# Grouping two pairs of row tiles in a one-core fused QKV projection: bf16 products together, float32r products together

## The chip, the cores and the metric

The kernel runs on one core of one Trainium2 chip. The metric is device time in microseconds (us) of one execution; the kernel before takes 360.74 us (median of 3 runs, 360.47 to 361.23). TensorE multiplies, VectorE, ScalarE and GpSimd (DVE, ACT and POOL in the profile) prepare operands and move results, and SyncE (SP) only issues DMAs.

## The reference

```python
batch, seq, hidden = 16, 512, 768          # x: 16 x 512 x 768, w_qkv: 768 x 2304, float32
qkv = np.matmul(x, w_qkv)
q, k, v = qkv[..., :768], qkv[..., 768:1536], qkv[..., 1536:]
return np.stack([q, k, v], axis=0)
```

So it is one matrix product of 8192 x 768 by 768 x 2304, whose columns go to three outputs.

## The kernel before, in words

**Tiling.** The 8192 rows of x are 64 row tiles of 128 rows. Two neighbouring row tiles form a pair (`p`, 0 to 31). The 2304 columns are two blocks of 1024 columns and, between them, a remainder of 256 columns (`REM`). A `Quad` is one pair times one of the two 1024-column blocks (`q` = 0 or 1): a 2 x 2 arrangement of 128 x 512 output tiles c11, c12, c21, c22, kept in one SBUF tile `o`.

**Seven products instead of eight.** Each quad is computed by one level of Strassen's scheme in Winograd's form: the inner size 768 is cut into two halves of 384, and seven half-size products are made, each of three matmuls (384 = 3 x 128) with 512 columns. Products 1 and 2 use x and w themselves, rounded to bf16 (`xb`, `b1`). Products 3 to 7 use sums and differences, in float32r (`sr` for x, `t1` to `t4` and `b22` for w). The remainder is done directly, in bf16, with twelve matmuls of 256 columns per pair (`rem`, L304; `rem_row`, L297). So a pair has twelve bf16 matmuls of 512 columns, twelve of 256, and thirty float32r matmuls of 512.

**One product and what follows it (`do`, L255).** Product 1 starts PSUM bank `u.x`, and ACT copies it out (`evacuate`, L253) while the bank stays in use; product 2 goes to bank `u.z`, which DVE adds to c11 (L266); product 6 accumulates into `u.x`, and ACT copies c12 (L269); product 5 starts bank `u.y`; product 7 accumulates into `u.x`, ACT copies c22 (L275) and DVE adds `u.y` (L276); product 4 accumulates into `u.x`, ACT copies c21 (L279); product 3 accumulates into `u.y`, which DVE adds to c12 (L282). There are 8 PSUM banks.

**Order of the work.** The schedule is written by hand: every engine runs its instructions in the order in which the program names them. After a start-up part (pairs 0 to 2 and the preparation of w), the loop at L602 takes pairs 3 to 31 one by one. For each pair `two` (L318) makes, for its quads a and b, in this order: a1, b1, `early()`, the remainder, a2, b2, a6, b6, a5, a7, b5, b7, a4, a3, store of a, b4, b3, store of b. `early` prepares the next pair (`ahead`, L486): `transpose` on DVE (L148, instruction at L154), `round_x` on POOL (L189, L191: the bf16 copy), `sums_x` on POOL (L204: five operations); then it issues the x load of the pair after that (`load_x`, L142): four DMAs, two on SP's queue and, from pair 5 on, two on ACT's queue (L129). Pair 31 goes through `last` (L360), whose products and stores are interleaved and which stores each quad in pieces (`store_cols`, L347) as they become ready, most on SP's queue and some on ACT's.

**Buffers that matter.** `o` tiles: 5; x as loaded (`xin`): 3; x transposed (`xf`): 2; bf16 x (`xb`): 4; sums of x (`s`): 2. One more quad-sized tile, `both`, holds w data at the start and later quad u2 (pair 2, second block, L598). Stores of a quad (`store_quad`, L287) are two DMAs on SP's queue (L289 and L290, or L293 and L294); the remainder's store is one (L314). In the built program every DMA issued from SP or ACT carries one of eight semaphores in turn, and waits until the DMA eight places earlier has landed.

Of the kernel before, what the change touches and what calls it, by code (L numbers as in the profile page):

```python
# [10 lines left out]
def kernel(  # L11
# [20 lines left out]
    nc = tc.nc  # L32
    P = 128
    G = 32
# [7 lines left out]
    NP = M // (2 * P)  # L42
# [18 lines left out]
    bt_pool = ctx.enter_context(tc.tile_pool(name="bt", bufs=1))  # L61
# [22 lines left out]
    both = bt_pool.tile([P, 2, KH * CB], fp32, name="both", tag="both")  # L84
# [41 lines left out]
    def load_x_half(p, h, eng):  # L126
        rows = x_flat[p * 2 * P:(p + 1) * 2 * P, :].rearrange("(g b) k -> b g k", b=G)
        for i in (2 * h, 2 * h + 1):
            eng.dma_start(xin[p][i * G:(i + 1) * G], rows[:, :, i * KC:(i + 1) * KC])  # L129
# [12 lines left out]
    def load_x(p, other):  # L142
        xin[p] = xin_pool.tile([P, 2 * P // G, KC], fp32, name="xin")
        load_x_half(p, 0, nc.sync)
        if other is not None:
            load_x_half(p, 1, other)

    def transpose(p, parts=1):  # L148
        t = xf_pool.tile([P, KT, 2 * P], fp32, name="xf")
        turned = t[:].rearrange("p j (g b) -> p g j b", b=G)  # L150
        rows = xin.pop(p)[:].rearrange("p g (a j) -> p g j a", a=G)
        n = 2 * P // G // parts
        for g in range(0, 2 * P // G, n):
            nc.vector.transpose(turned[:, g:g + n], rows[:, g:g + n])  # L154
        xf[p] = t

# [32 lines left out]
    def round_x(p):  # L189
        xb[p] = xb_pool.tile([P, KT, 2 * P], bf16, name="xb", tag="xb")  # L190
        nc.gpsimd.tensor_copy(out=xb[p][:], in_=xf[p][:])  # L191
# [12 lines left out]
    def sums_x(p, eng=None):  # L204
        t = xf.pop(p)
        a11, a12 = t[:, :KH, :P], t[:, KH:, :P]
        a21, a22 = t[:, :KH, P:], t[:, KH:, P:]
        s = s_pool.tile([P, 5, KH, P], f32r, name="s")
        sr[p] = s
        sums = {  # L210
            1: lambda g: g.tensor_tensor(s[:, 1], a21, a22, op=add),  # L211
            2: lambda g: g.tensor_tensor(s[:, 2], s[:, 1], a11, op=sub),  # L212
            3: lambda g: g.tensor_tensor(s[:, 3], a11, a21, op=sub),  # L213
            0: lambda g: g.tensor_copy(out=s[:, 0], in_=a22),
            4: lambda g: g.tensor_tensor(s[:, 4], a12, s[:, 2], op=sub),  # L215
        }
# [32 lines left out]
    def bank():  # L249
        return ps_pool.tile([P, CB], fp32, name="ps")  # L250

    def evacuate(u):
        nc.scalar.activation(u.o[:, 0, :CB], u.x[:], ident)  # L253

    def do(u, n, out=True):  # L255
        c11, c12 = u.o[:, 0, :CB], u.o[:, 0, CB:]
        c21, c22 = u.o[:, 1, :CB], u.o[:, 1, CB:]
        if n == 1:
            u.x = bank()
            product(u, 1, u.x, True)  # L260
            if out:
                evacuate(u)
        elif n == 2:
            u.z = bank()
            product(u, 2, u.z, True)
            nc.vector.tensor_tensor(c11, c11, u.z[:], op=add)  # L266
        elif n == 6:
            product(u, 6, u.x, False)
            nc.scalar.activation(c12, u.x[:], ident)  # L269
        elif n == 5:  # L270
            u.y = bank()
            product(u, 5, u.y, True)
        elif n == 7:
            product(u, 7, u.x, False)
            nc.scalar.activation(c22, u.x[:], ident)  # L275
            nc.vector.tensor_tensor(c22, c22, u.y[:], op=add)  # L276
        elif n == 4:
            product(u, 4, u.x, False)
            nc.scalar.activation(c21, u.x[:], ident)  # L279
        elif n == 3:  # L280
            product(u, 3, u.y, False)
            nc.vector.tensor_tensor(c12, c12, u.y[:], op=add)  # L282

    def rows_of(s, p, lo, hi):
        return out_flat[s, p * 2 * P:(p + 1) * 2 * P, lo:hi].rearrange("(r m) n -> m r n", m=P)

    def store_quad(u):  # L287
        if u.q == 0:
# [15 lines left out]
    def rem(p, eng=nc.sync, between=None):  # L304
        ps = ps_pool.tile([P, 2, REM], fp32, name="ps")
        rem_row(p, 0, ps[:, 0, :])
        if between is not None:
            between()
        rem_row(p, 1, ps[:, 1, :])

        def copied():
            o = or_pool.tile([P, 2, REM], fp32, name="orem")
            act.activation(o[:], ps[:], ident)  # L313
            return lambda: eng.dma_start(rows_of(1, p, R_OFF - H, R_OFF - H + REM), o[:])  # L314

        return copied

    def two(a, b, early, u=None):  # L318

        do(a, 1)  # L320
        do(b, 1, u is None)
        if u is None:
            early()
            rem(a.p)()()
        else:
            middle(u)
            copied = rem(a.p, between=lambda: third(u))
            evacuate(b)
            early()
            copied()()  # L330
            fourth(u)
        do(a, 2)
        do(b, 2)
        do(a, 6)
        do(b, 6)
        do(a, 5)
        do(a, 7)
        do(b, 5)
        do(b, 7)
        do(a, 4)  # L340
        do(a, 3)
        store_quad(a)
        do(b, 4)
        do(b, 3)
        store_quad(b)

    def store_cols(u, r, lo, hi, eng):  # L347

        c = Q_OFF[u.q] + lo
        end = Q_OFF[u.q] + hi  # L350
        while c < end:
            n = min(end, (c // H + 1) * H)
            row = (2 * u.p + r) * P
            eng.dma_start(  # L354
                out_flat[c // H, row:row + P, c % H:c % H + n - c],
                u.o[:, r, c - Q_OFF[u.q]:n - Q_OFF[u.q]],
            )
            c = n

    def last(a, b):  # L360

        p = a.p

        def rem_stored(r):
            ps = bank()
            rem_row(p, r, ps[:, :REM])
            o = or_pool.tile([P, 2, REM], fp32, name="orem")
            nc.scalar.activation(o[:, 0, :], ps[:, :REM], ident)  # L368
            row = (2 * p + r) * P
            nc.scalar.dma_start(out_flat[1, row:row + P, R_OFF - H:R_OFF - H + REM], o[:, 0, :])  # L370

        do(a, 1)
        do(b, 1)
        do(a, 2)
        do(a, 6)
        do(b, 2)
        do(b, 6)
        for u in (a, b):
            store_cols(u, 0, 0, CB, nc.sync)
        for u in (a, b):  # L380
            do(u, 5)
            do(u, 7)
            store_cols(u, 1, CB, 2 * CB, nc.sync)
        do(a, 4)
        store_cols(a, 1, 0, CB, nc.scalar)
        rem_stored(0)
        do(b, 4)
        store_cols(b, 1, 0, CB, nc.scalar)
        for u in (a, b):
            do(u, 3)  # L390
            store_cols(u, 0, CB, 2 * CB, nc.sync)
        rem_stored(1)


    ND = 2
# [21 lines left out]
    for h in range(2):  # L417
        rows = w_qkv.rearrange("(p j) n -> p j n", j=KT)[:, h * KH:(h + 1) * KH]
# [17 lines left out]
    quads = {}  # L436
# [34 lines left out]
    def middle(u):  # L471
        do(u, 6)
        do(u, 5)
        act.activation(u.o[:, 1, CB:], u.y[:], ident)
# [7 lines left out]
    def fourth(u):  # L482
        do(u, 4)
        store_quad(u)

    def ahead(p):  # L486
        transpose(p)
        round_x(p)
        sums_x(p)
# [7 lines left out]
    turned = [turn_row(0, 0)]  # L497
# [57 lines left out]
    u = quad(2, 0)  # L555
# [42 lines left out]
    u2 = quad(2, 1, bt_pool, "both")  # L598
    do(u2, 1)
    do(u2, 2)  # L600

    for p in range(ND + 1, NP):  # L602
        def early():
            if p + 1 < NP:
                ahead(p + 1)
            if p + 2 < NP:
                load_x(p + 2, nc.sync if p <= ND + 2 else nc.scalar)

        a, b = quad(p, 0), quad(p, 1)
        if p == ND + 1:  # L610
            two(a, b, early, u2)
        elif p < NP - 1:
            two(a, b, early)
        else:
            last(a, b)


# [28 lines left out]
```

## Time and profile before

| What | Value |
|---|---|
| median of 3 runs | 360.74 us (360.47 to 361.23) |
| the profiled execution's own time | 361.78 us |
| its span (first to last instruction) | 360.0 us |
| granted TensorE clock | 1.00 throughout |
| PE busy | 351.5 us (98%) |
| DVE, ACT, POOL busy | 227.8, 185.9, 178.8 us |
| HBM read, written | 32.28 MB, 75.50 MB |
| share of the 16 DMA engines' time: SP's queue, ACT's queue | 82.5%, 8.9% |

Busy shares are averages over the span. A matmul's end in the trace is modelled, and matmuls overlap: the distance from the start of one matmul to the start of the next is what it costs, not its duration (a 128x512 matmul lasts 379 to 399 ns in the groups, and another starts some 0.22 us later). A few matmul records are missing from the trace. "PEld" is TensorE's weight load, which runs beside the matmul before it. In a timeline, neighbouring equal instructions are merged into one row: its start, its length, and how many they are.

### The profile page before, as it was taken

Reading aid. Unit: us, or ns where it says so; the run is one execution under the profiler, and the core shown is the slowest. Engines: PE = TensorE matmul, PEld = TensorE weight load, DVE = VectorE, ACT = ScalarE, POOL = GpSimd, SP = SyncE. Lnnn points to the kernel's source line nnn. Section 1 sums busy time; section 2 is a strip of 40 time slices with the busy share of each in tenths; the row PEclk is TensorE's granted clock in tenths of the full one; section 3 lists DMA queues with packets and bytes.
Section 4 is the critical chain, followed back from the end, with each engine's and each line's share of the span. In section 5 each row is a group of like instructions: output and inputs, shape, how many; then the busy total and the mean of one; then the engine's idle time right before and its main releaser. Section 6 shows DMA issues by size and latency. Waiting matters only on the chain.

```text
span 360.0 us, 5248 instructions
## 1 busy us (share of the span) xinstructions
PE 351.5 (98%) x1749; PEld 251.4 (70%) x1780; DVE 227.8 (63%) x244; ACT 185.9 (52%) x316; POOL 178.8 (50%) x187
## 2 busy tenths in 40 slices
PE   7999999999999999999999999999999999999995
PEld 3465577777777777777777777777777777777764
DVE  2789676766566675566675566675556676556643
ACT  5469744545454545454545444455444445545443
POOL 0221856446664445665445665444665444665420
PEclk9999999999999999999999999999999999999999
DMA  7999999799998999899999899998999999989767
GB/s 265 340 367 345 325 357 371 236 333 298 275 325 301 295 276 290 282 319 301 292 285 284 284 309 309 292 285 282 290 295 315 293 295 272 297 283 322 291 238 257
DMA packets 82106, 107.73 MB, mean 299 GB/s; under 512 B 5408, under 2 KB 62240, under 8 KB 82080
## 3 DMA queue, kind: packets, MB, share of 16 engines
q1 hardware_dynamic: 66672, 96.35, 82.5%
q10 hardware_dynamic: 14608, 10.65, 8.9%
q0 software_dynamic: 800, 0.39, 0.8%
q8 instruction: 14, 0.23, 0.3%
q14 instruction: 12, 0.10, 0.1%
HBM read 32.28 MB, written 75.50 MB: 299 GB/s over the span
## 4 chain that ended last, share of the span: by engine, by line
PE 92%; DMA 5%; issue 1%; ACT 1%; ACTq 0%; POOL 0%; SPq 0%
PE ps L244 78%; PE ps L299 11%; PE ps L456 3%; DMA w_rem<-in_w_qkv_dram 2%; DMA xin<-in_x_dram 2%; DMA st<-in_w_qkv_dram 1%; ACT o L279 0%; ACTq L354 0%; POOL w_rem L419 0%; SPq L163 0%; ACT orem L368 0%; POOL mark L414 0%; ACTq L370 0%; ACTq L368 0%
## 5 line engine op out<-in xcount | busy, mean ns | idle before, releaser
L244 PE MATMUL ps<-t,s 128*128 128x512 f32 x720 | 181.2, 399 | 0.0
L244 PEld LDWEIGHTS ps<-t,s 128*128 128x128 f32 x720 | 135.0, 188 | 30.7
L191 POOL CAST xb<-xf 128x1536 bf16<-128x1536 f32 x28 | 41.0, 1464 | 132.2 <-DVE xf L154 132.2
L276 DVE TENSOR_TENSOR o<-o,ps 128x512 f32<-128x512 f32 x58 | 39.9, 688 | 91.5 <-ACT o L275 91.5
L154 DVE STREAM_TRANSPOSE xf<-xin 128x1536 f32<-128x1536 f32 (+1 forms) x32 | 88.7, 2775 | 1.7 <-DMA xin<-in_x_dram 1.7
L244 PE MATMUL ps<-b,xb 128*128 128x512 bf16 x331 | 85.3, 380 | 1.5
L244 PEld LDWEIGHTS <-xb 128*128 128x128 bf16 x360 | 32.8, 98 | 37.3 <-issue 7.6
L269 ACT ACTIVATE o<-ps 128x512 f32<-128x512 f32 x60 | 36.0, 600 | 43.6 <-PE ps L244 40.9
L275 ACT ACTIVATE o<-ps 128x512 f32<-128x512 f32 x58 | 34.7, 599 | 44.2 <-PE ps L244 44.2
L282 DVE TENSOR_TENSOR o<-o,ps 128x512 f32<-128x512 f32 x60 | 41.3, 688 | 21.4 <-PE ps L244 20.2
L244 PE MATMUL ps<-b,s 128*128 128x512 f32 x180 | 50.4, 389 | 0.0
L279 ACT ACTIVATE o<-ps 128x512 f32<-128x512 f32 x60 | 35.9, 598 | 24.6 <-PE ps L244 21.7
L253 ACT ACTIVATE o<-ps 128x512 f32<-128x512 f32 x60 | 35.8, 597 | 24.4 <-DVE o L282 20.7
L299 PE MATMUL ps<-w_rem,xb 128*128 128x256 bf16 x384 | 47.5, 273 | 0.6 <-DMA w_rem<-in_w_qkv_dram 0.6
L299 PEld LDWEIGHTS <-xb 128*128 128x128 bf16 x384 | 37.2, 98 | 12.3 <-issue 1.8
L266 DVE TENSOR_TENSOR o<-o,ps 128x512 f32<-128x512 f32 x60 | 37.8, 672 | 2.0 <-ACT o L253 1.3
L244 PEld LDWEIGHTS ps<-b,s 128*128 128x128 f32 x180 | 33.8, 188 | 7.1
L211 POOL TENSOR_TENSOR s<-xf 128x384 fp32r<-128x384 f32 x29 | 30.9, 1065 | 0.0
L212 POOL TENSOR_TENSOR s<-s,xf 128x384 fp32r<-128x384 f32 x29 | 29.4, 1015 | 2.3
L213 POOL TENSOR_TENSOR s<-xf 128x384 fp32r<-128x384 f32 x29 | 29.5, 1017 | 0.0
L215 POOL TENSOR_TENSOR s<-xf,s 128x384 fp32r<-128x384 f32 x29 | 29.5, 1017 | 0.0
L313 ACT ACTIVATE orem<-ps 128x512 f32<-128x512 f32 x31 | 18.5, 598 | 21.0 <-PE ps L299 21.0
(45 smaller groups left out, 119.3 us busy)
## 6 DMA issues: line engine op xcount, KB each, us to landing
out_dram<-o SPq DMA_DIRECT2D x62, 768.0 KB, 4.6
out_dram<-o SPq DMA_DIRECT2D x65, 256.0 KB, 4.0
xin<-in_x_dram SPq DMA_DIRECT2D x62, 192.0 KB, 6.9
xin<-in_x_dram ACTq DMA_DIRECT2D x50, 192.0 KB, 4.3
out_dram<-orem SPq DMA_DIRECT2D x31, 256.0 KB, 5.8
st<-in_w_qkv_dram SPq DMA_DIRECT2D x11, 256.0 KB, 5.6
st<-in_w_qkv_dram SPq DMA_DIRECT2D x3, 768.0 KB, 9.2
xin<-in_x_dram SPq DMA_DIRECT2D x4, 384.0 KB, 4.7
```

The source lines that it names most:

```text
L154: nc.vector.transpose(turned[:, g:g + n], rows[:, g:g + n])
L191: nc.gpsimd.tensor_copy(out=xb[p][:], in_=xf[p][:])
L211: 1: lambda g: g.tensor_tensor(s[:, 1], a21, a22, op=add),
L244: nc.tensor.matmul(ps[:], lhs[j], rhs[j], start=(start and j == 0), stop=(j == KH - 1), skip_group_check=True,)
L253: nc.scalar.activation(u.o[:, 0, :CB], u.x[:], ident)
L266: nc.vector.tensor_tensor(c11, c11, u.z[:], op=add)
L269: nc.scalar.activation(c12, u.x[:], ident)
L275: nc.scalar.activation(c22, u.x[:], ident)
L276: nc.vector.tensor_tensor(c22, c22, u.y[:], op=add)
L279: nc.scalar.activation(c21, u.x[:], ident)
L282: nc.vector.tensor_tensor(c12, c12, u.y[:], op=add)
L299: nc.tensor.matmul(ps, xb[p][:, j, r * P:(r + 1) * P], w_rem[j // KH][:, j % KH, :], start=(j == 0), stop=(j == KT - 1), skip_group_check= ...
```

## The change

From pair 6 on, two pairs form a group (13 groups: pairs 6 and 7, up to 30 and 31). A group makes all bf16 work of both pairs first (products 1 and 2 and the remainders), then the float32r products of the first pair's quads, then those of the second pair's. The group's first quad takes the tile `both`, the other three take `o` tiles. The order of the float32r products inside a pair stays as it was (`rounded`, the second half of the former `two`).

x is loaded four and five pairs ahead in a group (two pairs ahead before), always with all four DMAs on SP's queue. So that the first group finds its data, pair 3 loads two pairs' x (5 and 6), pair 4 loads x of pair 7, pair 5 loads x of 8 and 9, and pair 5 also does the transpose of pair 7, in two halves put between the stores and additions of its float32r products, and its rounding. Inside a group the transposes and roundings of the next two pairs stand in the bf16 part, and `sums_x` runs for the group's second pair at the group's start and for the next group's first pair in the middle.

In the last group the remainder of pair 31 stays at the end, in `last`; products 1 and 2 leave `last`, and so do the places of products 6: they now stand one after the other. The first store pieces of pair 31 come before them in the program.

The core of the diff:

```diff
-    def two(a, b, early, u=None):
+    def two(a, b, early, u=None, turns=()):
...
         do(a, 2)
         do(b, 2)
+        rounded(a, b, turns)
+
+    def rounded(a, b, turns=()):
         do(a, 6)
         do(b, 6)
         do(a, 5)
         do(a, 7)
         do(b, 5)
         do(b, 7)
+        for t in turns[:1]:
+            t()
         do(a, 4)
         do(a, 3)
         store_quad(a)
+        for t in turns[1:]:
+            t()
         do(b, 4)
         do(b, 3)
         store_quad(b)
...
-        do(a, 1)
-        do(b, 1)
-        do(a, 2)
-        do(a, 6)
-        do(b, 2)
-        do(b, 6)
         for u in (a, b):
             store_cols(u, 0, 0, CB, nc.sync)
+            do(u, 6)
...
+    def group(p):
+        quads = [quad(p, 0, bt_pool, "both"), quad(p, 1)]
+        do(quads[0], 1)
+        do(quads[1], 1)
+        sums_x(p + 1)
+        if p + 2 < NP:
+            transpose(p + 2)
+            round_x(p + 2)
+        if p + 4 < NP:
+            load_x(p + 4, nc.sync)
+        rem(p)()()
+        do(quads[0], 2)
+        do(quads[1], 2)
+        quads += [quad(p + 1, q) for q in range(2)]
+        do(quads[2], 1)
+        do(quads[3], 1)
+        if p + 5 < NP:
+            load_x(p + 5, nc.sync)
+        if p + 2 < NP:
+            rem(p + 1)()()
+        do(quads[2], 2)
+        do(quads[3], 2)
+        if p + 3 < NP:
+            transpose(p + 3)
+            round_x(p + 3)
+        rounded(*quads[:2])
+        if p + 2 < NP:
+            sums_x(p + 2)
+            rounded(*quads[2:])
+        else:
+            last(*quads[2:])
...
-        if p == ND + 1:
-            two(a, b, early, u2)
-        elif p < NP - 1:
-            two(a, b, early)
-        else:
-            last(a, b)
+    NG = ND + 4
+    extra = {NG - 3: (NG, ), NG - 1: (NG + 3, )}
+    for p in range(ND + 1, NG):
+        late_turns = []
+        def early():
+            ahead(p + 1)
+            for n in (p + 2 + (p > NG - 3), ) + extra.get(p, ()):
+                load_x(n, nc.sync)
+            if p == NG - 1:
+                late_turns.extend(transpose(NG + 1, 2, True))
+        two(quad(p, 0), quad(p, 1), early, u2 if p == ND + 1 else None, late_turns)
+        if p == NG - 1:
+            round_x(NG + 1)
+    for p in range(NG, NP, 2):
+        group(p)
```

`transpose(p, 2, True)` returns the two half transposes as functions, to be called later.

More of the change, by code (lines that the diff above doesn't have):

```diff
@@ L146, in load_x, with transpose @@
             load_x_half(p, 1, other)
-    def transpose(p, parts=1):
+    def transpose(p, parts=1, split=False):
         t = xf_pool.tile([P, KT, 2 * P], fp32, name="xf")
@@ L152, in transpose @@
         n = 2 * P // G // parts
-        for g in range(0, 2 * P // G, n):
-            nc.vector.transpose(turned[:, g:g + n], rows[:, g:g + n])
+        turns = [
+            lambda g=g: nc.vector.transpose(turned[:, g:g + n], rows[:, g:g + n])
+            for g in range(0, 2 * P // G, n)
+        ]
         xf[p] = t
+        if split:
+            return turns
+        for turn in turns:
+            turn()
     def load_row(p, r):
@@ L600 @@
     do(u2, 2)
-    for p in range(ND + 1, NP):
-        def early():
[L604 to L609, printed above, removed]
-        if p == ND + 1:
-            two(a, b, early, u2)
-        elif p < NP - 1:
-            two(a, b, early)
-        else:
-            last(a, b)
+    def group(p):
[33 more added lines that the diff above has]
+        late_turns = []
+        def early():
+            ahead(p + 1)
[8 more added lines that the diff above has]
+        group(p)
 _INS = ['x', 'w_qkv']
```

## The prediction

> **What bounds the kernel now.** First the page: who is busy, and in which slices.
>
> ```profile
> span 360.0 us, 5248 instructions
> PE 351.5 (98%) x1749; PEld 251.4 (70%) x1780; DVE 227.8 (63%) x244; ACT 185.9 (52%) x316; POOL 178.8 (50%) x187
> PE   7999999999999999999999999999999999999995
> DMA  7999999799998999899999899998999999989767
> PE 92%; DMA 5%; issue 1%; ACT 1%; ACTq 0%; POOL 0%; SPq 0%
> ```
>
> PE is busy in every slice but the first and the last, and the chain of work that ended last is 92% PE. The DMA engines are almost as full, so they are the second limit to watch. Next, PE's timeline over one pair, and VectorE's over the same time:
>
> ```profile
> 151.85 1.47 PE L244 MATMUL ps<-b,xb 128*128 128x512 bf16 x6
> 153.16 1.47 PE L299 MATMUL ps<-w_rem,xb 128*128 128x256 bf16 x12
> 154.47 1.46 PE L244 MATMUL ps<-b,xb 128*128 128x512 bf16 x5
> 155.57 5.14 PE L244 MATMUL ps<-t,s 128*128 128x512 f32 x21
> 160.55 0.84 PE L244 MATMUL ps<-b,s 128*128 128x512 f32 x3
> ...
> 162.59 1.47 PE L244 MATMUL ps<-b,xb 128*128 128x512 bf16 x6
> ```
> ```profile
> 152.65 2.94 DVE L154 STREAM_TRANSPOSE xf<-xin 128x1536 f32<-128x1536 f32 x1
> 155.51 1.25 DVE L266 TENSOR_TENSOR o<-o,ps 128x512 f32<-128x512 f32 x2
> 159.34 0.69 DVE L276 TENSOR_TENSOR o<-o,ps 128x512 f32<-128x512 f32 x1 [2.58 <-ACT o L275]
> ```
>
> A pair lasts 162.59 - 151.85 = 10.74 us, without a wait on PE, and all starts of remainders from 56.50 to 335.74 lie 10.74 us apart: there is no stall to remove. Inside it I take the distances of single starts in the trace: bf16 216 ns, remainder 109.2 ns, float32r 226.65 ns once steady. 12 x 216 + 12 x 109.2 + 30 x 226.65 = 10,702 ns; the other 39 ns are the **round trip between the types**: from float32r to bf16 the last distance is 230 and the first bf16 one 226 (together +14), and after bf16 the first seven float32r matmuls take 1,612 ns where seven steady ones take 1,587 (+25).
>
> Last, the end, by stretches of time (columns: stretch, length, busy times, clock, DMA share, GB/s):
>
> ```profile
> 345.00:348.00 3.00, 3.00 (x15) 1.48 (x14) 1.31 (x2) 1.48 (x3) 0.00 (x0) 1.00 0.80 311
> 348.00:352.00 4.00, 4.00 (x19) 3.21 (x18) 1.39 (x3) 1.79 (x3) 0.00 (x0) 1.00 1.05 401
> 352.00:353.00 1.00, 1.00 (x8) 0.67 (x7) 0.33 (x2) 0.82 (x2) 0.00 (x0) 1.00 0.30 105
> 353.00:355.00 2.00, 2.00 (x12) 1.67 (x11) 0.58 (x2) 1.04 (x3) 0.00 (x0) 1.00 0.72 266
> 355.00:358.00 3.00, 1.15 (x9) 0.56 (x7) 1.21 (x2) 0.70 (x2) 0.00 (x0) 1.00 0.98 354
> ```
>
> The DMA engines idle between 341.2 and 345.6, run full at about 400 GB/s until 352.3, and have gaps again until 355. PE's stream ends at 355.99 (last start 355.88 + 0.109), DMA traffic at about 358.6, the span at 360.0.
>
> **The steady groups: -0.55 us.** Removed are round trips. Before, from pair 6 on: 25 pairs with one each, and three in pair 31 (its rows show bf16, float32r, bf16, float32r, remainder, float32r, remainder). After: 13 groups with one each, and one around the first half remainder at the end. 28 - 14 = 14 round trips of 39 ns = 0.55 us. The matmuls themselves, their sizes and their number stay.
>
> The rest is whether anything now makes PE wait. I lay a group on the rows above, T = 0 at its first product, 21.44 us long: bf16 until 7.80, the first pair's float32r until 14.60. The order of the built program tells which PSUM bank follows which.
> - VectorE: the previous group's last addition ends at 0.9, a transpose runs to 3.8, then the additions of product 2 of the first two quads to 4.3 and 4.9 (655 and 690 ns). The banks that they free are needed again at 6.5 (third quad's product 2) and 9.2 (first product 5): 2.2 us and more to spare. The second transpose, 8.7 to 11.7, delays the first L276 addition by 0.3 us, which nothing on PE waits for before 14.6.
> - POOL: sums of the second pair 0.1 to 4.6 (4.51 + gaps by L211 to L215), roundings until 6.1 and 13.2, sums of the next first pair 14.7 to 19.2. First needed at 14.6, 21.4, 25.3 and 29.2.
> - `both`, the one single buffer: a first quad's store is issued 10.33 us into its pair today (L289, 162.18), in a group 3.9 us later for the second pair's bf16 work, at 14.2; ACT writes the tile again at about 22.3. L289 and L290 land 3.3 to 6.4 us after issue: 17.5 to 21.
> - x: its eight DMAs are issued between 2.5 and 10.5 (0.74 to 1.4 us each on SP's full queue), land about 7 us later, and are needed at 22.3 and 30. Today they land at about 162.2 for a transpose at 163.39, so the move from two queues to SP's alone is covered. The wait for the DMA eight places back costs SP time only; the first store of the group, at 14.2, waits for an x load landed by 10.5. DMA volume: a pair keeps the engines busy about 9.4 us of 10.74, a group about 18.8 of 21.44, so each half drains before the next stores.
> So the steady part hides everything, and I put its waits at nothing.
>
> **Into the first group: +0.25 us (0 to 0.5).** In pair 5 the two half transposes (1.53 to 1.58 us in the L154 rows) stand among the additions: 9.50 to 11.0, addition to 11.7, 11.65 to 13.2 from the pair's start. POOL then rounds (L191, 1.46 us) until 14.7; with some 0.1 us for the signal, `xb` of pair 7 is there at 14.8. PE wants it at 10.74 + 3.90 = 14.64, and its weight load 0.1 to 0.2 earlier. I take 0.25. The early loads of x 6 and 9 move 0.79 MB each forward into pairs 3 to 5; DMA idles there around 70 to 72 us (97 GB/s), and the stores that they delay have a pair of spare `o` tiles: nothing.
>
> **The end: +0.85 us (0 to +1.3).** Pair 30's quads used to be stored a whole pair before the end; now `last` holds only float32r products and half remainders, so they come later. From the end of pair 30's last product to the end of PE's stream it was 355.99 - 345.17 = 10.82 us; now it is 7 x 0.68 + 0.655 + 3 x 0.68 + 0.655 + 0.05 = 8.16 us. DMA traffic began 0.48 us after that product (345.65), so now it begins 7.68 us before the stream's end. To move are pair 30's two quads and all of pair 31's output: the per-microsecond figures from 345 to 359 sum to 4.46 MB, and the new end has the same. At 400 GB/s that is 11.15 us without a gap: traffic ends 3.47 us after PE's stream, against 358.62 - 355.99 = 2.63 before. The gaps that the old end had (1.8 us in 12.97) are used up. ACT's and SP's issues stay in time, since each piece waits in line anyway.
> Nearest rows for the bounds: single full microseconds run from 380 to 419 GB/s. At 385 the end costs +1.3, at 419 +0.35; below that, nothing, if the pieces overlap better than I see.
> The Trainium skill ("DMA: Bandwidth & Descriptors", Specifications) gives 435 GB/s as the ceiling of the 16 engines. No full microsecond here reaches it (419 at most); at that figure the 4.46 MB would take 10.25 us, the end would cost nothing, and the sum below would be an estimated -0.35 us instead of +0.55.
>
> **Sum:** -0.55 + 0.25 + 0.85 = +0.55 us: 362.3 for the profiled execution (361.78), which lies 1.04 above the median; against the median, 361.3. A measurement of this kernel can tell about 0.2% (0.72 us) from no change, so I forecast no change that shows.
>
> **Rivals.**
> - *The end is hidden* (drain at 419 GB/s or more): -0.55 + 0.25 + 0 to 0.35, that is 360.4 to 360.8. For it: 409 to 419 in several microseconds. Against it: 401 over the longest full stretch.
> - *The end weighs more*, and the result is slower: with 0.25 at the first group the end must cost 1.02 us to cross 0.72, which is a drain at 394 GB/s or less, or a start 0.2 us later. The 380, 385 and 390 GB/s rows and the smaller pieces at the end (364 GB/s at share 0.99) speak for it: 361.5 to 362.1.
> - *`both` comes free late*: ACT is in order, so the first evacuation of each group would hold the second, and the additions behind it. It decides once the store lands over 10 us after issue (8.1 us to the next write, then the 2.2 us that the bank has to spare); each us beyond costs 13 us: 363 or more. The longest landing of a quad's store is 8.2 us, at the start of the kernel; usual are 3.4 to 6.4.
> - *It doesn't separate the types on PE*: excluded, the built program's PE order shows one change each way in a group.
> - *Faster by over 0.72 us* needs more than all round trips (0.55 us) and a free end; no row gives it, so only what I don't see.
>
> **How the numbers follow.** Forecast (361.0 to 361.45) 0.41, hidden end 0.16, heavier end 0.25, `both` or another wait in the groups 0.09, faster 0.09. Same: 0.41 + 0.16 = 0.57; slower: 0.25 + 0.09 = 0.34; faster 0.09. The range goes from -0.55 (all round trips, no cost: 360.2) to -0.55 + 0.5 + 1.3 = +1.25, and some 0.03 us of waiting in each group (+0.4): 362.4.
>
> **What would show it.** Right: pairs' PE rows repeat every 21.44 us (two old pairs are 21.48), PE's stream ends 0.3 to 0.55 us sooner, at 355.4 to 355.7; no DMA gap from the first store of pair 30 to the end, with traffic ending about 3.5 us after PE. Wrong: a group longer than 21.48 us (a wait: which bank or tile does the matmul name?), a wait of PE for POOL's `xb` well over 0.5 us near 77 to 81 us, or gaps in the last 12 us of DMA.

## The result: slower by 0.4%, and the profile after

The kernel after takes 362.60 us (median of 5 runs, 362.27 to 363.09) where the kernel before took 360.74 beside it. The measured ratio is 1.0043, with an interval of 1.0032 to 1.0055 (the quotient of the two medians, 1.0052, lies inside it). That is +1.55 us (360.74 x 0.0043; +1.15 to +1.98), where the forecast was +0.55 and "no change that shows". The profiled execution took 362.47 us; that it lies near the 362.3 forecast for it is luck, since its start-up was 0.66 us shorter than that of before.

The page of the kernel after, the lines that answer to those of before:

```profile
span 360.7 us, 5246 instructions
PE 353.1 (98%) x1780; PEld 252.1 (70%) x1780; DVE 230.6 (64%) x245; ACT 185.9 (52%) x316; POOL 178.0 (49%) x187
PE   7999999999999999999999999999999999999994
DMA  7999999999899898979989899898989989846648
PE 92%; DMA 6%; POOL 0%; ACT 0%; SPq 0%; issue 0%; ACTq 0%
```

The page hardly moves: PE is still busy in all slices but the first and the last, and the chain is 92% PE. Two marks are new. The last PE slice fell from 5 tenths to 4 while the last DMA slice rose from 7 to 8, and the chain has 6% DMA instead of 5%: the transfers now outlast PE by more.

The start of the kernel must be taken out before two executions are compared; up to the point used here, the change only brings loads of x forward. Pair 4's first remainder matmul begins at 56.50 us in the trace of before and at 55.84 in that of after. (The expectation of before_again calls it pair 3's. But pair 6, the first of the first group, has its remainder at 77.32 in after, two steps of 10.74 us later, and pair 3's begins at 43.6 in before.) Over the 14 profiled executions of this study it began anywhere from 55.46 to 57.12, the kernel before alone at 56.50 and 55.69. In the two traces compared here the difference is that of the first loads: on the chain that ended last, the load of `w_rem` ends at 20.83 us in before and at 20.18 in after. So I cut each execution there, and again at the last matmul's start. Outside the span lie 1.8 us in both traces.

| | before | after | difference | predicted |
|---|---|---|---|---|
| pair 4's first remainder to the last matmul | 299.38 us | 299.24 us | -0.14 | -0.30 |
| last matmul to the end of the span | 4.08 us | 5.61 us | +1.53 | +0.85 |
| sum | 303.46 us | 304.85 us | +1.39 | +0.55 |

The first row repeated to 0.01 us in the traces of kernels that share it (299.38 in three traces: before, before once more, and before with another queue for x); so did the second (4.08 in each). So each step can be read from its own stretch.

**A group.** PE's timeline of the kernel after, one group (start, length, engine, line, operation):

```profile
161.99 1.47 PE L250 MATMUL ps<-b,xb 128*128 128x512 bf16 x6
163.30 1.47 PE L305 MATMUL ps<-w_rem,xb 128*128 128x256 bf16 x12
...
169.61 5.14 PE L250 MATMUL ps<-t,s 128*128 128x512 f32 x21
174.59 0.86 PE L250 MATMUL ps<-b,s 128*128 128x512 f32 x3
175.29 0.85 PE L250 MATMUL ps<-t,s 128*128 128x512 f32 x3
175.98 0.84 PE L250 MATMUL ps<-b,s 128*128 128x512 f32 x3
176.66 4.92 PE L250 MATMUL ps<-t,s 128*128 128x512 f32 x21
181.42 0.84 PE L250 MATMUL ps<-b,s 128*128 128x512 f32 x3
182.10 0.84 PE L250 MATMUL ps<-t,s 128*128 128x512 f32 x3
```

The types are separated as the diff says: one row of bf16, then one of float32r. But the first product 3 of the group, at 174.59, lasts 0.86 us instead of 0.84, and the next product begins 0.70 us after it instead of 0.68 (the second pair's, at 181.42, keep 0.84 and 0.68). From 174.36 on, a row of float32r matmuls stands up to 236 ns apart, instead of 226.65. It is a second slowed row of matmuls, like the one that follows bf16, in a place where no type changes. VectorE over the same time:

```profile
169.41 1.34 DVE L272 TENSOR_TENSOR o<-o,ps 128x512 f32<-128x512 f32 x2 [2.47 <-ACT orem L319]
170.66 3.07 DVE L154 STREAM_TRANSPOSE xf<-xin 128x1536 f32<-128x1536 f32 x1
173.62 0.69 DVE L282 TENSOR_TENSOR o<-o,ps 128x512 f32<-128x512 f32 x1
174.74 0.69 DVE L282 TENSOR_TENSOR o<-o,ps 128x512 f32<-128x512 f32 x1 [0.43 <-ACT o L281]
```

The group's second transpose ends at 173.73 (170.66 + 3.07), and the addition of c22 (L282; L276 of before) comes right behind it and ends at 174.3. Product 3 accumulates into the bank that this addition reads, `u.y`, so its weight load waits for it:

```profile
173.46 0.87 PEld L250 LDWEIGHTS ps<-t,s 128*128 128x128 f32 x4
174.42 0.59 PEld L250 LDWEIGHTS ps<-b,s 128*128 128x128 f32 x3
```

The load at 174.42 starts 61 ns after the matmul that it runs beside (174.36), where a load of the steady row starts 3 ns after its matmul. (The semaphore instruction ahead of it lasts 51 ns, held or not, so that length doesn't tell the wait.) In the trace of before the same addition ended at 160.03 (159.34 + 0.69), 0.52 us before its product 3 (160.55), whose load starts 4 ns after its matmul.

A rival is GpSimd: its rounding of x (L197) begins right behind the second transpose and runs beside the slowed row. The kernel after itself speaks against it, in the next group:

```profile
195.25 1.47 POOL L197 CAST xb<-xf 128x1536 bf16<-128x1536 f32 x1 [5.70 <-DVE xf L154]
196.06 0.84 PE L250 MATMUL ps<-b,s 128*128 128x512 f32 x3
```

The rounding lies where it lay before, but here product 3 keeps its 0.84 us, no distance there exceeds 227 ns, and the group lasts 21.44 us; the weight load starts 44 ns behind its matmul. So does one more group of after (43 ns). The other groups from the second to the twelfth, in after and in the kernels below that keep this order, have loads 52 to 88 ns behind and a slowed row.

**Into the first group.** PE's timeline of after, the third and fourth quads of the group of pairs 6 and 7:

```profile
78.63 2.87 PE L250 MATMUL ps<-b,xb 128*128 128x512 bf16 x12
```

The same twelve matmuls take 2.75 us at 164.61: one distance of 318 ns in place of 216, at 79.71, where `xb` of pair 7 is awaited. It costs 0.10 us.

**The end.** Stretches of the kernel after (columns as in the prediction: stretch, length, busy times, clock, DMA share, GB/s):

```profile
347.00:348.00 1.00, 1.00 (x6) 0.82 (x5) 0.69 (x1) 0.24 (x2) 0.00 (x0) 1.00 0.52 212
348.00:358.00 10.00, 7.36 (x39) 5.56 (x37) 2.75 (x4) 4.26 (x8) 0.00 (x0) 1.00 1.06 395
358.00:359.00 1.00, 0.00 (x0) 0.00 (x0) 0.00 (x0) 0.00 (x0) 0.00 (x0) 1.00 0.81 296
```

The drain is as predicted in kind: it begins at 347.5, 7.7 us before PE's stream ends, has no gap, and moves 4.46 MB (0.212 + 10 x 0.395 + 0.296). The last transfer ends 4.05 us after the last matmul's start, where it was 2.83 in before. But that explains only 1.22 of the 1.53 us, and the 1.22 is more than the 0.84 that the same working had given.

### The profile page after: what moved, and what is told of

Its sections match the earlier page's. It is cut to its first block, busy times and chain, and to the rows that moved or that the text cites. A ratio compares the mean times of both kernels' runs of the same rounds, so it can differ in the third digit from the quotient of the medians.

```text
span 360.7 us, 5246 instructions
## 1 busy us (share of the span) xinstructions
PE 353.1 (98%) x1780; PEld 252.1 (70%) x1780; DVE 230.6 (64%) x245; ACT 185.9 (52%) x316; POOL 178.0 (49%) x187
## 4 chain that ended last, share of the span: by engine, by line
PE 92%; DMA 6%; POOL 0%; ACT 0%; SPq 0%; issue 0%; ACTq 0%
PE ps L250 78%; PE ps L305 11%; PE ps L465 3%; DMA w_rem<-in_w_qkv_dram 2%; DMA xin<-in_x_dram 2%; DMA st<-in_w_qkv_dram 1%; DMA out_dram<-o 1%; POOL w_rem L428 0%; SPq L169 0%; ACT o L285 0%; POOL mark L423 0%; ACT orem L382 0%; ACTq L368 0%; ACTq L382 0%
## 5 line engine op out<-in xcount | busy, mean ns | idle before, releaser
L250 PE MATMUL ps<-t,s 128*128 128x512 f32 x720 | 178.2, 395 | 0.0
L154 DVE STREAM_TRANSPOSE xf<-xin 128x1536 f32<-128x1536 f32 (+1 forms) x33 | 91.1, 2763 | 1.2 <-DMA xin<-in_x_dram 1.1
L197 POOL CAST xb<-xf 128x1536 bf16<-128x1536 f32 x28 | 41.1, 1466 | 80.2 <-DVE xf L154 80.2
L282 DVE TENSOR_TENSOR o<-o,ps 128x512 f32<-128x512 f32 x58 | 39.9, 688 | 60.2 <-ACT o L281 60.2
L250 PEld LDWEIGHTS <-xb 128*128 128x128 bf16 x360 | 33.8, 98 | 37.1 <-issue 4.2
L305 PEld LDWEIGHTS <-xb 128*128 128x128 bf16 x384 | 37.2, 98 | 11.9 <-issue 1.4
```

What stands on the lines that cost most here:

```text
L154: lambda g=g: nc.vector.transpose(turned[:, g:g + n], rows[:, g:g + n])
L250: nc.tensor.matmul(ps[:], lhs[j], rhs[j], start=(start and j == 0), stop=(j == KH - 1), skip_group_check=True,)
L305: nc.tensor.matmul(ps, xb[p][:, j, r * P:(r + 1) * P], w_rem[j // KH][:, j % KH, :], start=(j == 0), stop=(j == KT - 1), skip_group_check= ...
```

## The experiments

Each kernel's ratio is against the kernel before on the same chip, with its 95% interval. The table at the end of this section has the stretches of each trace. Theories, formed after the result: **A**, pair 30's stores, now late, fill the DMA engines at the end (the prediction's own reason). **B**, the waits inside the groups: the second transpose holds the addition of c22. **C**, formed when A had failed to explain one kernel, and tested from two_queues on: the change moves x's DMAs between the instruction streams of ACT and SP, and so moves the fetching of code blocks into the last microseconds.

**before_again**: the kernel before, unchanged.

> The kernel before once more, unchanged, to see how much its start-up varies from one profiled execution to the next. The first profile of before began the remainder of pair 3 at 56.50 us, the profile of the changed kernel at 55.84, though nothing up to there differs but two loads of x. If the start-up alone varies, the ratio is 1.000 within 0.001, every pair from 3 on again takes 10.74 us, and pair 3 may begin up to 1 us earlier than in the first profile. If the changed kernel's earlier start came from its own loads, pair 3 begins at 56.5 again.

1.0003 of the kernel before (0.9993 to 1.0012). The stretch from pair 4's remainder on is 299.38 us and the end 4.08 us, as in the first trace; the start was 0.81 us shorter. So the 1.04 us by which the first profiled execution lay above its median were mostly its start.

**end_old**: groups up to pair 29 only; pairs 30 and 31 as before the change.

```diff
-        if p + 2 < NP:
-            sums_x(p + 2)
-            rounded(*quads[2:])
-        else:
-            last(*quads[2:])
+        sums_x(p + 2)
+        rounded(*quads[2:])
...
-    for p in range(NG, NP, 2):
+    for p in range(NG, NP - 2, 2):
         group(p)
+    two(quad(NP - 2, 0), quad(NP - 2, 1), lambda: sums_x(NP - 1))
+    last(quad(NP - 1, 0), quad(NP - 1, 1))
```

(Products 1, 2 and 6 go back into `last` as well.)

> The changed kernel, but with groups only up to pair 29; pairs 30 and 31 run as in the kernel before. Theory A (the time went into the end, where pair 30's stores come late and the DMA engines set the end): the end from PE's last start to the span's end falls from 5.6 back to about 4.1 us, the steady part keeps its 0.02 us per group, less 0.1 us at the first group; ratio to before 0.999 to 1.001. Theory B (the groups cost time in the middle, for instance by x on one queue, in executions without a profile): ratio stays at 1.003 or more.

1.0041 (1.0027 to 1.0055): undoing the grouped end alone brings nothing back. A as the only cause falls. The end is 5.07 us, a microsecond more than in before, though the last two pairs are made as in before and pair 30's stores come early; and the groups last 21.50 us, 0.02 more than two old pairs.

**end_only**: the kernel before with only the last two pairs grouped.

```diff
+    for p in range(ND + 1, NP - 2):
...
+            if p == NP - 4:
+                load_x(NP - 1, nc.scalar)
+            if p == NP - 3:
+                late_turns.extend(transpose(NP - 1, 2, True))
...
+    group(NP - 2)
```

> The kernel before up to pair 28 and in pair 29 nearly so (it also transposes pair 31), with only the last two pairs made as a group, x on two queues as before. Theory A: the end from PE's last start to the span's end is about 5.5 us, against 4.1, and the ratio to before is 1.003 to 1.0045. Theory B: ratio 1.000 to 1.001, since there is one group only.

1.0062 (1.0047 to 1.0076). The end is 5.25 us: the grouped end by itself costs 1.17 us. The ratio holds more than that: the half transposes that I put into pair 29 make a stall of 0.44 us there (that pair lasts 11.18 us), and 2.14 us instead of 1.8 lie outside the span (as in turn_early, 2.12), for which I have no reason. Neither is the change's: the trace of after has no such stall and 1.8 us outside.

**switch_more**: in the kernel before, product 6 of the first quad goes ahead of product 2 of the second, so each pair changes type twice more.

```diff
         do(a, 2)
-        do(b, 2)
         do(a, 6)
+        do(b, 2)
         do(b, 6)
```

> The kernel before with one more change between bf16 and float32r in each of pairs 3 to 30: product 6 of the first quad is put before product 2 of the second, as in the last pair. If a round trip between the types costs what I read (39 ns, or about 28 ns where only three float32r matmuls stand between), a pair takes 10.77 to 10.78 us instead of 10.74, and the sum is +0.8 to +1.1 us: ratio 1.002 to 1.003. If the slow matmuls behind a switch come from something else in the pair (POOL's rounding at the same time), a pair stays at 10.74 us and the ratio at 1.000.

1.0013 (1.0003 to 1.0022). PE's timeline of this kernel, around the added switch:

```profile
154.22 0.81 PE L244 MATMUL ps<-b,xb 128*128 128x512 bf16 x3
154.68 1.04 PE L244 MATMUL ps<-t,s 128*128 128x512 f32 x3
155.57 0.82 PE L244 MATMUL ps<-b,xb 128*128 128x512 bf16 x3
156.04 4.44 PE L244 MATMUL ps<-t,s 128*128 128x512 f32 x18
```

The pair lasts 10.76 us instead of 10.74: about 20 ns for the added round trip, 0.54 us over the stretch (299.92 against 299.38). Changing type does cost, but less than the 0.8 us expected for the kernel, and less than the 39 ns of the sum when only three float32r matmuls stand between: the slowed row is cut short.

**two_queues**: the kernel after, with half of each x load of a group on ACT's queue again.

```diff
-            load_x(p + 4, nc.sync)
+            load_x(p + 4, nc.scalar)
...
-            load_x(p + 5, nc.sync)
+            load_x(p + 5, nc.scalar)
```

> The kernel after, but with the second half of each x load of a group on ACT's queue again, as before the change. Measured from the last matmul's start to the end of the span, the kernel before has 4.08 us, the kernel after 5.60. Theory C (the x loads lengthen SP's own instruction stream, whose code blocks of 8 KB are then fetched in the last microseconds; after has such fetches at 341.7, 357.7 and 360.9 us, before none later than 309.3 on that queue): this end shrinks to 4.4 to 4.9 us, no fetch in the last 10 us, time some 0.8 us below after. Theory A (pair 30's late stores, 4.46 MB to drain): the end stays at 5.4 to 5.6 us, time as after, within 0.3 us. Theory B (a wait inside the groups) says nothing of the end; the 21.46 us of a group stay.

1.0033 (1.0021 to 1.0046); end 5.31 us, 0.30 less than after, not the 0.7 and more that C had claimed, and more than A allowed. Both have a part. The queues in the last microseconds, 353 us on, first of after and then of two_queues (second row: GB/s by slices):

```profile
GB/s 393 377 381 389 410 393 414 373 373 381 402 402 410 365 389 377 377 381 426 389 410 352 369 53 12 0 0 0 0 0 0 33 0 0 0 0 0 0 0 0
q1 hardware_dynamic: 1238, 1.45, 40.1%
q10 hardware_dynamic: 720, 0.79, 21.9%
q14 instruction: 2, 0.02, 0.5%
```
```profile
GB/s 410 348 373 397 406 414 393 377 361 389 393 426 401 353 393 373 381 385 393 418 401 377 320 8 0 0 0 0 0 0 0 0 0 0 0 0 0 0 0 0
q1 hardware_dynamic: 1229, 1.44, 39.6%
q10 hardware_dynamic: 720, 0.79, 21.9%
```

The kernel after fetches two blocks of code (8 KB each, the queue named "instruction") at 357.7 and 360.9 us, after the last matmul; the second is the lone 33 GB/s near the end of its row. That one begins 0.25 us after the span has ended (360.69), so only the first can weigh on the end. In two_queues that queue moves nothing in the window; its last block came at 314.7 us.

**end_old_two**: end_old, with x in the groups on both queues (the edit of two_queues).

> Groups up to pair 29 only, pairs 30 and 31 as in the kernel before, and now x in the groups on both queues; with x on SP's queue alone the same kernel had an end of 5.07 us (before: 4.08), though its last two pairs are made as before, and groups of 21.50 us. Theory C: with SP's stream short again the end falls to 4.1 to 4.3 us, and no code block is fetched in the last 10 us. Theory A alone has no reason for the 5.07 and none for a change: 5.0 to 5.1. If the queue that x takes also sets when things happen inside a group, the period moves from 21.50 us; Theory B as it stands (DVE's order) leaves it at 21.46 to 21.50.

0.9998 (0.9988 to 1.0008), and the end is 4.08 us, that of before. So the extra microsecond of end_old comes with the queue of x, not with any store. The same view of both, 353 us on; end_old first:

```profile
core 0 of [0], span 361.6 us
...
q14 instruction: 2, 0.02, 0.5%
```
```profile
core 0 of [0], span 359.3 us
...
q1 hardware_dynamic: 640, 0.84, 22.6%
q10 hardware_dynamic: 720, 0.79, 21.9%
```

There is no line of queue 14 in the second. In end_old SP issues the last but one store 0.60 us after the last matmul and it lands at 3.41; in end_old_two 0.57 and 2.84. ACT makes its last copy 0.27 us later (at 0.66 instead of 0.39) and issues the last store as much later (1.07, 0.80); it lands at 3.73 and 3.17. And SP's closing instruction takes until 4.24 instead of 3.26: it begins 0.34 us after SP's last wait for a landing, where 0.04 us lay between.

**no30**: the kernel after without pair 30's four quad stores (that part of the output is not written).

```diff
     def store_quad(u):
+        if u.p == NP - 2:
+            return
```

> The kernel after without the four quad stores of pair 30 (2.1 MB of the output are not written). Theory A (the late stores of pair 30 fill the DMA engines at the end): the end, from the last matmul's start, falls from 5.60 to 4.1 us or less, time 1.3 to 1.6 us below after. Theory C (late fetches of SP's code): SP's stream is only four DMAs shorter, the fetches stay in the last microseconds, and the end stays above 4.7 us; under both, the landings of the last stores need 2.3 us again instead of 3.2 to 3.5.

1.0020 (1.0010 to 1.0030); end 4.88 us, above the 4.7 of C and not the 4.1 of A, with a block of code fetched 1.90 us after the last matmul (another follows only after the span). So taking away the drain saves 0.73 us, taking away the late fetches (two_queues) saves 0.30, and each leaves a rest: the two causes overlap. It also shows that the groups' length is not fixed: up to pair 29 this is the program of after, yet nine of its first twelve groups last 21.50 us, where after's last 21.44 to 21.48 from the second on.

**turn_early**: the kernel after, with the second transpose and rounding of a group ahead of products 2 of the second pair.

```diff
-        do(quads[2], 2)
-        do(quads[3], 2)
         if p + 3 < NP:
             transpose(p + 3)
             round_x(p + 3)
+        do(quads[2], 2)
+        do(quads[3], 2)
```

> The kernel after, but with the group's second transpose and rounding named before products 2 of the second pair's quads, so that the transpose lies in the bf16 part and not in front of the first addition to c22. Theory B (that addition ends late, and product 3, which accumulates into the bank it reads, has its weight load held, after which some seven float32r matmuls start 230 ns apart instead of 226.6): the second slow run near 12.4 us of a group vanishes, a group lasts 21.44 instead of 21.46 us, and from pair 3 to the last matmul it is 0.2 to 0.3 us less than after's 299.25. Rival: the transpose then delays the additions of product 2, whose banks the products 5 need, and the slow run only moves, so that the group stays at 21.46 or grows. The end stays at 5.6 us either way.

1.0059 (1.0045 to 1.0074), a miss for the whole kernel: in the first group the earlier transpose waits 1.23 us for POOL's sums of pair 7 (made late there, and the last to read the tile `xf` that it writes), the additions queue up behind it, and PE stands still for 0.62 us at 89.44. From the second group on B holds, in each group. VectorE and then PE of turn_early:

```profile
168.50 2.97 DVE L154 STREAM_TRANSPOSE xf<-xin 128x1536 f32<-128x1536 f32 x1
171.38 1.26 DVE L272 TENSOR_TENSOR o<-o,ps 128x512 f32<-128x512 f32 x2
175.01 0.69 DVE L282 TENSOR_TENSOR o<-o,ps 128x512 f32<-128x512 f32 x1 [2.37 <-ACT o L281]
```
```profile
171.24 5.14 PE L250 MATMUL ps<-t,s 128*128 128x512 f32 x21
176.22 0.84 PE L250 MATMUL ps<-b,s 128*128 128x512 f32 x3
176.90 0.84 PE L250 MATMUL ps<-t,s 128*128 128x512 f32 x3
177.58 0.84 PE L250 MATMUL ps<-b,s 128*128 128x512 f32 x3
178.26 4.92 PE L250 MATMUL ps<-t,s 128*128 128x512 f32 x21
```

The addition now ends at 175.70, 0.52 us before product 3, and waits for ACT alone. Product 3 takes 0.84 us again, the 30 float32r matmuls of the first pair take 7.02 us (171.24 to 178.26) where after needed 7.05, and every group from the second on lasts 21.44 us, as the sum of the prediction had it.

**before_sp**: the kernel before, with x on SP's queue alone.

```diff
-                load_x(p + 2, nc.sync if p <= ND + 2 else nc.scalar)
+                load_x(p + 2, nc.sync)
```

> The kernel before with one part of the change alone: every x load wholly on SP's queue, nothing else. Theory C (x on SP's queue lengthens SP's instruction stream by some 50 DMAs and moves the fetches of its 8 KB code blocks): such fetches appear in the last 10 us, and the end, from the last matmul to the end of the span, grows from 4.08 to 4.9 to 5.1 us, as in end_old. Theory A: nothing at the end changes, 4.1 us. If the one queue also brings x late, a wait of PE on POOL's xb shows in the pairs and they last longer than 10.74 us; the prediction held that covered (landing 1.2 us ahead of the transpose).

0.9997 (0.9986 to 1.0008), end 4.08, pairs 10.74: as the prediction held, the queue itself is free. C's expectation missed: the last blocks are fetched at 338.7 and 341.2 us, not in the last 10 us. That narrows C: it isn't SP's queue that costs, but a block that falls due after the last matmul. I counted the instructions of each engine that the traces show ahead of every such fetch. Blocks come as ACT's count reaches about 66, 194, 323 and 450 (443 to 452), that is every 128, and at 84 to 87, 210 to 213, 337 to 345 and again in its last instructions at 461 to 468 of SP's. ACT has 529 in all in before, 478 in before_sp, but 453 in after and 455 in end_old; SP 405, 455, 466 and 468. So only in the last two do both engines meet a mark in their last few instructions (in after, SP's block then comes when SP has done its last).

**two_early**: two_queues, with the early transpose of turn_early from the second group on.

```diff
-        do(quads[2], 2)
-        do(quads[3], 2)
+        if p == NG:
+            do(quads[2], 2)
+            do(quads[3], 2)
         if p + 3 < NP:
             transpose(p + 3)
             round_x(p + 3)
+        if p > NG:
+            do(quads[2], 2)
+            do(quads[3], 2)
```

> The kernel after without what theories B and C blame: x on both queues, and from the second group on the second transpose before products 2 of the second pair. What is left of its cost is the end by theory A and the first group. Groups 21.44 us; from pair 3 to the last matmul 0.3 to 0.4 us less than before (299.38), so 299.0; end 5.3 us as in two_queues. Sum some 0.8 us over before, ratio 1.0015 to 1.003. If the parts are not additive, the end differs from 5.3 by more than 0.15.

1.0019 (1.0010 to 1.0028): the stretch from pair 4's remainder on is 299.02 us, -0.36, and the end 5.25, +1.17. With B and C gone, what is left of the change's cost is A.

**best**: end_old_two with the same early transpose, so without A, B and C.

> Groups up to pair 29 only, pairs 30 and 31 as before the change, x on both queues, and from the second group on the second transpose early: none of A, B, C is left. Groups 21.44 us instead of 21.48, twelve of them, so 0.45 us less, 0.1 us lost at the first group: from pair 3 to the last matmul 299.0 us (before 299.38); end 4.1 us. Ratio 0.999, at the edge of what can be told. If the switch between the types were not the 39 ns that the sum used, the groups would not be 21.44 us.

0.9993 (0.9982 to 1.0003): groups of 21.44 us, end 4.09. The stretch is 299.23, not 299.0, because the first group lasted 0.18 us longer than in two_early (its first transpose waited 0.28 us for x). The interval holds 1: it takes the loss away and can't be told from the kernel before.

**end_old_pad**: end_old with 24 instructions more on SP and on ACT.

```diff
+    pad = w_pool.tile([P, 24, 8], fp32, name="pad")
+    def padded(n):
+        nc.sync.dma_start(pad[:, n], x_flat[n * P:(n + 1) * P, :8])
+        nc.scalar.activation(tiny[:], eye[:, :1], ident)
...
             load_x(p + 4, nc.sync)
+        padded(p - NG)
...
             load_x(p + 5, nc.sync)
+        padded(p - NG + 1)
```

> The kernel end_old (groups to pair 29, x on SP's queue alone, end 5.07 us) with 24 tiny loads of 128 x 8 numbers on SP's queue and 24 one-column activations on ACT, two of each in every group, whose results nothing reads. In the traces so far a block of code is fetched whenever ACT's count of instructions passes 66, 194, 322 and 450, and SP's 84 to 87, 212, 337 to 345 and 466 to 468. The 24 instructions more carry both counts past these marks some 24 instructions before the end. Theory C: no such fetch after the last matmul; the end, from the last matmul's start, is 4.1 to 4.3 us as in the kernel before, although more work and more DMAs are done. If it isn't the fetches but the queue that x took (order of DMAs or of their semaphores; 24 is a multiple of the eight semaphores), the end stays at 5.0 to 5.1 us. The groups may grow by some ns.

1.0009 (0.9998 to 1.0020), end 4.21 us instead of 5.07, with more work done. SP's block is now fetched at 348.5 us, as its count reaches 469 of 492. ACT's traced count grew only to 457, and its block comes as it reaches 449, at 355.9: 0.1 us after the last matmul and not well ahead of it as expected. So the extra microsecond goes with where the streams end and not with x's queue. Which engine's block it is stays open: SP's and ACT's moved together, and VectorE's traced count changed too (430, from 452 in end_old).

| kernel | from pair 4's remainder to the last matmul, us | end, us | last transfer after the last matmul, us | code fetched more than 1 us after it | ratio |
|---|---|---|---|---|---|
| before_again | 299.38 | 4.08 | 2.83 | no | 1.0003 |
| after | 299.24 | 5.61 | 4.05 | yes | 1.0043 |
| two_queues | 299.59 | 5.31 | 3.79 | no | 1.0033 |
| two_early | 299.02 | 5.25 | 3.79 | no | 1.0019 |
| turn_early | 299.80 | 5.60 | 4.05 | yes | 1.0059 |
| end_only | 299.84 | 5.25 | 3.79 | no | 1.0062 |
| no30 | 299.62 | 4.88 | 3.30 | yes | 1.0020 |
| end_old | 299.72 | 5.07 | 3.30 | yes | 1.0041 |
| end_old_pad | 299.52 | 4.21 | 2.97 | no | 1.0009 |
| end_old_two | 299.64 | 4.08 | 2.83 | no | 0.9998 |
| best | 299.23 | 4.09 | 2.83 | no | 0.9993 |
| before_sp | 299.38 | 4.08 | 2.82 | no | 0.9997 |
| switch_more | 299.92 | 4.09 | 2.83 | no | 1.0013 |

## Why the prediction's sum was too small, step by step

The sum pointed the right way and was 1.0 us too small: +0.55 against +1.55. The likeliest case, no change that shows, did not come by the prediction's own mark of 0.72 us. The rival that the end weighs more did, beyond the 361.5 to 362.1 us that it gave, and without the drain at 394 GB/s or less that it named. That +1.55 still lies under the top of the range (+1.65, 362.4) is in part luck: the end went over its own bound of +1.3, and room left for the first group and for waits made up for it.

- **The round trips, -0.55 us: right in size, but not reached.** Without the wait a group lasts 21.44 us, the predicted figure (turn_early, two_early, best), and two_early has -0.36 in the stretch, where twelve such groups give -0.48 and the first group takes back 0.15 (21.59 us). In the kernel after itself the groups last 21.46 us on average in its trace, and mostly 21.50 in no30, two_queues and end_old: so between -0.02 and +0.02 a group.
- **"So the steady part hides everything": this step failed.** The prediction saw that the second transpose delays the first L276 addition by 0.3 us and said that "nothing on PE waits for" it "before 14.6". I had asked when the bank comes free for a new product. But product 3 accumulates into that same bank, its weight load is due at 12.4 us of the group, and it waits for the addition to have read it. The wait itself is short (the load comes 43 to 88 ns behind its matmul); what costs is the slowed row of matmuls, most of them 229 to 240 ns apart, behind it. Its length changes with some 10 ns of shift (nothing at 44 ns, 24 to 62 ns in sum at 53), which is why the groups differ from one to the next. So the waits put at nothing cost up to 0.06 us a group (21.50 against 21.44), where the round trip that is saved gives 0.04.
- **The first group, +0.25 us: right in kind,** 0.10 measured, inside its bounds.
- **`both`, x from one queue: right.** No stall by either in the groups of after; before_sp is as fast as before. (The 9.4 us of DMA work in a pair was read too low: the DMA share from 151.85 to 162.59 is 0.93, or 10.0 us. Nothing came of it.)
- **The end, +0.85 us: the drain was right and its price too small.** Without late fetches it costs 1.17 to 1.23 us (end_only, two_early, two_queues). The start of the drain (7.7 us before the stream's end) and its 4.46 MB were as worked out. The rate was 395 GB/s and not 400, and the last transfer ends 0.96 us later than before (3.79 against 2.83) where 0.84 was predicted. The other 0.2 us were not in the sum at all: SP closes the kernel by waiting for the last DMAs in a fixed order. In before they landed in that order and one wait was left after the last landing; in two_queues the first one waited for landed 3.29 us after the last matmul, and four waits, some 65 ns each, were left after the last landing at 4.21.
- **The rate that only a page gives.** The Trainium skill ("DMA: Bandwidth & Descriptors", Specifications) has 435 GB/s as the fabric ceiling, by which the end would have been free. No full microsecond of this drain passes 427, and its mean over 10 us is 395: for a drain of mixed pieces the measured mean decides.
- **The code blocks, +0.3 us: not in the prediction in any form.** I had argued that the move of x to one queue costs nothing if x comes in time. It does come in time; what the move changes is where ACT's and SP's streams end within their blocks of code. That the late block belongs to these two engines is inferred from the counts; that the extra time goes with it, and neither with the queue nor with the stores, is shown by end_old against end_old_two and end_old_pad. Whether the transfer itself costs the time, or the engine's standing still for its code, is not shown.

The sum, by the runs: -0.14 to +0.24 us in the steady part with the first group (by how the slowed rows fall: after and no30), +1.2 for the drain, +0.3 for the code: +1.4 to +1.7, and +1.55 was measured.

What stays open: how a fetch of 8 KB holds a landing back by 0.6 us (no30 and end_old issue the last but one store as early as end_old_two and see it land at 3.41 instead of 2.84), and why a load held so shortly is followed by slowed matmuls at all. Neither was tried by itself.

## What to carry to other kernels

When two phases are merged near the end of a kernel, add up the bytes that are stored after the merge point, divide by the rate measured over a long full stretch, and compare with what PE still has to do: here 4.46 MB stood against 7.7 us of matmuls. When work is moved on an engine, look for every later matmul that accumulates into a bank that the delayed instruction reads, not only for the one that starts the bank anew. And when a change of 0.5 us is sought, compare the stretches of the trace, not the totals, and look at the instruction queue's times in the last microseconds.

## What the runs showed of the hardware that was not expected

- Code is fetched while the kernel runs, in blocks of 8 KB on queue 14 and 16 KB on queue 8, the last of them more than 1 us after the last matmul in after, turn_early, no30 and end_old. A fetch 1.9 to 2.65 us after the last matmul went with an end that was 0.3 us (beside a full drain: after against two_queues) to 1.0 us (beside a short one: end_old against end_old_two) longer.
- A float32r weight load that starts 52 to 88 ns behind the matmul beside it, instead of 3, is followed by a row of matmuls (eleven in the longest, in end_old_pad) of which most stand 229 to 240 ns apart instead of 226.65, 14 to 69 ns in sum, even with no change of type; loads 43 and 44 ns behind (two groups of after) were followed by none.
- A round trip between bf16 and float32r costs 20 ns when it is added with three float32r matmuls inside (switch_more), and 39 ns with thirty (21.44 us a group instead of two pairs of 10.74).
